# Low parts of twelve input-projection weight tiles by ScalarE and an adding transfer, and eight conv slices a tile

## The chip, the core and the metric

The kernel runs on one core of a Trainium2 chip. The core has a matrix engine (TensorE, PE in the profile), a vector engine (VectorE, DVE), a scalar engine (ScalarE, ACT), a general engine (GpSimd, POOL), and a sync engine (SyncE, SP) that only issues transfers. Each engine works through its own list of instructions in order; semaphores between them say when an operand is ready or a buffer is free. The metric is the device time of one execution in microseconds (us). The kernel before takes 1417.85 us, the median of three runs from 1417.19 to 1418.00.

## The reference

A hybrid decoder layer over 1024 positions of width 1024, all in float32, cut here to the part that matters:

```
proj = rmsnorm(h) @ w_in            # columns: q 512 | k 512 | v 512 | u 1024
a = diff_attention(rope(q), rope(k), v, lam)      # 4 heads, causal, two softmax maps
c = u[:, :512] * sigmoid(u[:, 512:])              # gate
c = causal_dwconv(c, cv_dw_w) + cv_dw_b           # 512 channels, 31 taps
c = silu(layernorm(c))
h = h + concat([a, c]) @ w_out
h = h + cross_attention(...)                      # 4 heads, 256 memory tokens
h = h + conv_ffn(...)                             # gated, width 2816, 3 taps
return rmsnorm(h)
```

## The kernel before

**Products in three matmuls.** Each float32 operand is split into a part `hi`, rounded to the matrix engine's float32r format, and the rest, `lo = x - hi`. A product is `hi*lo + lo*hi + hi*hi`: three matmuls for each 128 x 128 block of weights and 512 columns (`mm3`, lines 198, 199, 200; the second one is the first to read a weight tile's `lo`).

**Input projection.** Sixteen weight tiles of 128 x 1024 (kind `in`, in the order `in_order`: 12, 8, 0, 1, 13, 9, 2, 3, 14, 10, 4, 5, 6, 7, 15, 11) are loaded from HBM by SyncE into `raw` (three buffers). ScalarE copies `raw` to `whi` (line 181), VectorE writes `wlo = raw - whi` (line 182); `whi` and `wlo` have two buffers each, so tile m+1's cast waits until TensorE has read tile m-1 for the last time. Then come four tiles of v (kind `v`), and the sixteen of the memory's keys and values (kind `kv`), which are multiplied beside the attention. Tiles 12 to 15 and 8 to 11 are the two halves of the conv's input; `gate` and `gated` (lines 489 to 499) multiply them, by a sigmoid on ScalarE. `qk_out` (line 504) takes q and k tiles out of PSUM.

**The conv.** `conv31` (line 352) is a generator for one of four channel tiles: some 50 slices, most of them a VectorE multiply-add of 128 x 512 in place (line 371), and at its start, end and middle lines 369 and 377 to 385. The generators, and that of the rotary tables (`rope_tables`, lines 390 to 449), stand in a list `bg`. `run_bg(NBG)` after each weight tile hands out `NBG` slices in turn, at a lowered priority; what is left is handed out before the attention by `run_bg(1000)`.

**Attention.** TensorE's order is fixed by hand in a loop over 32 units (`scores`, `turn`, `weigh`), with the memory's key and value products as filling work (`mem_kv`, line 613). All of `mem_kv` use one PSUM bank, `mb`: unit u+1 waits until unit u has been taken out of it, for the keys by VectorE at line 628. `qk_split` (line 667) splits each head's q and k into `hi` and `lo` (casts on ScalarE at lines 220 and 682, subtractions on VectorE at lines 221 and 683). The first head's split stands ahead of the loop. `maxima` (line 708) and `expo` (line 714) are the softmax.

**What sets the order.** TensorE's instructions keep the order of the code in the stretches under `manual_schedule`. The other engines' lists are put in order when the program is built, from priorities and estimated durations, and are fixed after that; so an edit at one line can shift others on the same engine.

Of the kernel before, what the change touches and what calls it, by code (L numbers as in the profile page):

```python
# [14 lines left out]
ALU = mybir.AluOpType  # L15
# [42 lines left out]
def hybrid_block_kernel(ctx: ExitStack, tc: tile.TileContext, xT, memT, pos, vecs, lams, ropec,  # L58
                        wi, wv, wo, wq, wkv, wc, wu, wd, gfin, outT, outB):
    nc = tc.nc  # L60
# [15 lines left out]
    def nm(s):  # L76
        cnt[0] += 1
        return f"{s}_{cnt[0]}"

    def R():  # L80
        return pt.tile([P, S], F32R, tag="t", name=nm("r"))
# [4 lines left out]
    def T(dt=F32):  # L86
        return pt.tile([P, S], dt, tag="t", name=nm("t"))
# [19 lines left out]
    def f(ap):  # L107
        return ap.bitcast(F32)
# [34 lines left out]
    in_order = [12, 8, 0, 1, 13, 9, 2, 3, 14, 10, 4, 5, 6, 7, 15, 11]  # L143
# [30 lines left out]
    def split_w():  # L174
        kind, m, mode, raw = loaded.pop(0)
        if mode == "rd":
            hi, lo = R(), R()
        else:
            hi = pw[0].tile([P, S], F32R, tag="whi", name=nm("whi"), bufs=2)
            lo = pw[0].tile([P, S], F32R, tag="wlo", name=nm("wlo"), bufs=2)  # L180
        nc.scalar.copy(out=hi, in_=raw)  # L181
        nc.vector.tensor_tensor(out=lo, in0=raw, in1=f(hi), op=ALU.subtract)  # L182
        prepped[(kind, m)] = (hi, lo)

    def need(kind, m, ahead=None):
# [5 lines left out]
    def load_to(i):  # L191
        while wpos[0] <= min(i, wend[0] - 1):
            load_w()
            split_w()
# [65 lines left out]
    for i in range(2):  # L260
        kind, m, src, _ = seq[wpos[0]]
        wpos[0] += 1
        raw = pw[0].tile([P, S], F32, tag="raw", name=nm("raw"), bufs=3)
# [67 lines left out]
    def run_bg(n):  # L331
        with tc.high_priority(offset=-500):
            while n > 0 and bg:
                g = bg.pop(0)
                if next(g, StopIteration) is not StopIteration:
                    bg.append(g)
                    n -= 1
# [117 lines left out]
    def rope(tiles):  # L455

        r = T()
        for h in range(NH):
            nc.scalar.dma_start(out=r[h * 32:(h + 1) * 32, :], in_=tiles[h][48:80, :])
        sw = T()  # L460
        nc.vector.stream_shuffle(out=sw, in_=r, mask=SWAP)
        nc.vector.tensor_tensor(out=r, in0=r, in1=cos_t, op=ALU.mult)
        nc.vector.tensor_tensor(out=sw, in0=sw, in1=sin_t, op=ALU.mult)
        nc.vector.tensor_tensor(out=r, in0=r, in1=sw, op=ALU.add)
        for h in range(NH):
            nc.scalar.dma_start(out=tiles[h][48:80, :], in_=r[h * 32:(h + 1) * 32, :])
# [38 lines left out]
                                           in1=rxb[:, sl], op0=ALU.mult, op1=ALU.mult)  # L505
        qk[m] = t

    NBG = 6

    with tc.manual_schedule(engines={mybir.EngineType.PE}):  # L510
        w, w2 = need("in", 12), need("in", 8, 0)
# [27 lines left out]
    for m in in_order[3:]:  # L539
# [6 lines left out]
        else:  # L546
            qk_out(m, [(slice(0, S), ps)])
            if m % 4 == 3:
                rope(qk[m - 3:m + 1])
        run_bg(NBG)  # L550
    vsb = [T() for _ in range(4)]

    def vproj():
# [3 lines left out]
        for i in range(4):  # L557
# [8 lines left out]
            if i < 3:  # L566
                run_bg(NBG)
        for tb in range(NB):
# [277 lines left out]
    next(prep)  # L846
    run_bg(NBG)

# [139 lines left out]
    for m in range(8):  # L988
# [8 lines left out]
        hi, lo = R(), R()  # L997
# [601 lines left out]
```

## Time and profile before

| | |
|---|---|
| median of three runs | 1417.85 us (1417.19 to 1418.00) |
| the profiled execution | 1418.36 us, of which its span is 1416.6 us |
| TensorE busy | 1378.1 us, 97% of the span |
| VectorE busy | 1066.8 us, 75% |
| ScalarE busy | 578.1 us, 41% |
| GpSimd busy | 211.2 us, 15% |
| mean granted TensorE clock | 0.994 of full speed |

The profile is of one execution. Busy shares are means over the whole span; stages differ much, so the rows further down are cut by stage. `PEclk` is the share of full speed that TensorE was granted in a stretch: 1.00 is 2.4 GHz and 0.50 is 1.2 GHz. In a timeline, the bracket behind a row is the idle time of that engine just before it and what ended that time. Matmuls overlap, so their durations may add up to more than the stretch they lie in. A name such as `cv` or `wlo` stands for all buffers of that name.

### The profile page before, as it was taken

How to read it: one execution, taken by the hardware profiler on the slowest of the kernel's cores; microseconds unless marked ns; L12 is line 12 of the kernel's file. 1: busy time of each engine (PE TensorE's matmuls, PEld its weight loads, DVE VectorE, ACT ScalarE, POOL GpSimd, SP SyncE). 2: the span in 40 equal slices, each digit the busy share in tenths (PEclk: the TensorE clock that was granted, in tenths of full speed). 3: DMA queues.
4: the chain of work that ended last, by engine and by line, in shares of the span. 5: the costliest groups of instructions: out<-in, count | busy, mean ns of one | idle time of the engine just before them, and what ended most of it. 6: DMA issues, size and time to landing. Idle time of an engine off the chain costs nothing.

```text
span 1416.6 us, 17449 instructions
## 1 busy us (share of the span) xinstructions
PE 1378.1 (97%) x6709; PEld 1148.2 (81%) x6709; DVE 1066.8 (75%) x1385; ACT 578.1 (41%) x1023; POOL 211.2 (15%) x169
## 2 busy tenths in 40 slices
PE   8999999898899999999999999999999999999998
PEld 6888887887787888888878787887887877888886
DVE  7799999999955424454688888988888897666636
ACT  6211135688763223343464444444443451221213
POOL 0000000013210000000134333443334400000000
PEclk9999999999999999999999999999999999999999
DMA  6132123432205422202421222222222274313103
GB/s 220 42 98 73 56 90 98 141 118 77 74 31 200 149 90 74 75 31 75 155 80 70 76 80 83 89 75 79 85 75 89 89 299 176 119 61 118 45 1 119
DMA packets 50196, 137.36 MB, mean 97 GB/s; under 512 B 6336, under 2 KB 8640, under 8 KB 50112
## 3 DMA queue, kind: packets, MB, share of 16 engines
q1 hardware_dynamic: 43904, 119.98, 25.2%
q10 hardware_dynamic: 6208, 16.26, 3.6%
q8 instruction: 53, 0.87, 0.2%
q14 instruction: 31, 0.25, 0.1%
HBM read 101.51 MB, written 28.41 MB: 92 GB/s over the span
## 4 chain that ended last, share of the span: by engine, by line
PE 61%; DVE 18%; issue 8%; ACT 7%; POOL 6%; DMA 1%; SPq 0%; POOLq 0%; ACTq 0%; DVEq 0%
PE big L198 16%; PE big L200 16%; PE big L199 16%; POOL t L1171 5%; DVE q L1323 4%; ACT q L1321 3%; PE tb L765 2%; DVE r L221 2%; PE bk L198 1%; DVE wu L221 1%; PE bk L200 1%; PE bk L199 1%; PE mb L198 1%; DVE q L1346 1%; DVE q L1298 1%
## 5 line engine op out<-in xcount | busy, mean ns | idle before, releaser
L199 PE MATMUL big<-r,wlo 128*128 128x512 f32 x624 | 243.7, 390 | 0.6 <-DVE wlo L182 0.6
L200 PE MATMUL big<-r,whi 128*128 128x512 f32 x624 | 243.7, 391 | 0.0
L198 PE MATMUL big<-r,whi 128*128 128x512 f32 x560 | 219.7, 392 | 3.1 <-DVE r L304 2.1
L181 ACT CAST whi<-raw 128x1024 fp32r<-128x1024 f32 x58 | 61.4, 1058 | 204.1 <-PE big L200 171.2
L199 PEld LDWEIGHTS big<-r,wlo 128*128 128x128 f32 x624 | 117.6, 188 | 24.8 <-DVE wlo L182 0.9
L200 PEld LDWEIGHTS big<-r,whi 128*128 128x128 f32 x624 | 117.4, 188 | 24.6
L1431 DVE TENSOR_TENSOR t<-t,big 128x1024 f32<-128x1024 f32 x70 | 85.4, 1220 | 61.9 <-PE big L200 61.8
L1323 DVE SCALAR_TENSOR_TENSOR q<-q,vec,q 128x1023 f32<-128x1023 f32 x88 | 112.6, 1280 | 19.9 <-ACT q L1321 19.8
L198 PEld LDWEIGHTS big<-r,whi 128*128 128x128 f32 x560 | 105.6, 189 | 27.0 <-DVE r L304 3.4
L198 PE MATMUL big<-r,r 128*128 128x512 f32 x312 | 121.8, 391 | 1.8 <-DVE t L1431 1.6
L199 PE MATMUL big<-r,r 128*128 128x512 f32 x312 | 121.5, 389 | 0.0
L200 PE MATMUL big<-r,r 128*128 128x512 f32 x312 | 121.5, 389 | 0.0
L198 PE MATMUL ub<-r,wu 128*128 128x512 f32 x302 | 119.0, 394 | 1.7 <-ACT half L1278 1.7
L199 PE MATMUL ub<-r,wu 128*128 128x512 f32 x302 | 117.6, 389 | 0.0
L200 PE MATMUL ub<-r,wu 128*128 128x512 f32 x302 | 117.6, 389 | 0.0
L1171 POOL TENSOR_TENSOR t<-uraw 128x512 f32<-128x512 f32 x22 | 48.4, 2199 | 389.3 <-DMA uraw<-in_wu_dram 167.1
L198 PE MATMUL ub<-r,t 128*128 128x512 f32 x228 | 90.0, 395 | 4.2 <-ACT half L1278 2.8
L199 PE MATMUL ub<-r,t 128*128 128x512 f32 x228 | 88.8, 390 | 0.0
L200 PE MATMUL ub<-r,t 128*128 128x512 f32 x228 | 88.8, 389 | 0.0
L371 DVE SCALAR_TENSOR_TENSOR cv<-t,vec,cv 128x511 f32<-128x511 f32 (+14 forms) x120 | 84.2, 743 | 0.0
L181 ACT CAST r<-raw 128x1024 fp32r<-128x1024 f32 x22 | 22.9, 1051 | 134.8 <-PE big L198 134.5
L182 DVE TENSOR_TENSOR wlo<-raw,whi 128x1024 fp32r<-128x1024 f32 x58 | 70.9, 1223 | 6.8 <-ACT whi L181 6.6
(340 smaller groups left out, 3047.8 us busy)
## 6 DMA issues: line engine op xcount, KB each, us to landing
uraw<-in_wu_dram SPq DMA_DIRECT2D x88, 256.0 KB, 2.9
z_dr<-q SPq DMA_DIRECT2D x22, 512.0 KB, 2.6
raw<-in_wd_dram SPq DMA_DIRECT2D x22, 512.0 KB, 3.7
t<-z_dr SPq DMA_DIRECT2D x22, 512.0 KB, 4.8
raw<-in_wkv_dram SPq DMA_DIRECT2D x16, 512.0 KB, 3.7
raw<-in_wi_dram SPq DMA_DIRECT2D x14, 512.0 KB, 3.7
t<-h_dr SPq DMA_DIRECT2D x9, 512.0 KB, 10.0
kv_dr<-r SPq DMA_DIRECT2D x8, 512.0 KB, 3.5
```

Of the source, the lines that this page charges most:

```text
L181: nc.scalar.copy(out=hi, in_=raw)
L182: nc.vector.tensor_tensor(out=lo, in0=raw, in1=f(hi), op=ALU.subtract)
L198: nc.tensor.matmul(out, wh, xl, start=start, stop=False, **kw)
L199: nc.tensor.matmul(out, wl, xh, start=False, stop=False, **kw)
L200: nc.tensor.matmul(out, wh, xh, start=False, stop=stop, **kw)
L221: nc.vector.tensor_tensor(out=lo, in0=src, in1=f(hi), op=ALU.subtract)
L371: nc.vector.scalar_tensor_tensor(out=y[:, i:], in0=x[:, :n2 - i], scalar=t, in1=y[:, i:], op0=ALU.mult, op1=ALU.add)
L765: nc.tensor.matmul(av, u["at"][:, bs(j)], vsb[j // 2][:, (j % 2) * HALF + h * P:][:, :P], start=j == 0, stop=j == qb)
L1171: nc.gpsimd.tensor_tensor(out=out, in0=a, in1=b, op=ALU.add)
L1321: nc.scalar.mul(t, u, tp[2])
L1323: nc.vector.scalar_tensor_tensor(out=t[:, d:], in0=u[:, :S - d], scalar=tp[2 - d], in1=t[:, d:], op0=ALU.mult, op1=ALU.add)
L1431: nc.vector.tensor_tensor(out=h2[m], in0=h2[m], in1=ps, op=ALU.add)
```

## The change

For the twelve `in` tiles behind the first four of `in_order`, the subtraction on VectorE goes. ScalarE writes minus `hi` into `wlo` (line 184), and a transfer that GpSimd issues (line 185) adds `raw` to it in place. The first four `in` tiles, and all tiles of other kinds, keep the subtraction. `NBG` goes from 6 to 8.

```diff
@@ -179,7 +179,12 @@
             hi = pw[0].tile([P, S], F32R, tag="whi", name=nm("whi"), bufs=2)
             lo = pw[0].tile([P, S], F32R, tag="wlo", name=nm("wlo"), bufs=2)
         nc.scalar.copy(out=hi, in_=raw)
-        nc.vector.tensor_tensor(out=lo, in0=raw, in1=f(hi), op=ALU.subtract)
+        if kind == "in" and m not in in_order[:4]:
+
+            nc.scalar.mul(lo, f(hi), -1.0)
+            nc.gpsimd.dma_start(out=f(lo), in_=raw, accum_op=ALU.add)
+        else:
+            nc.vector.tensor_tensor(out=lo, in0=raw, in1=f(hi), op=ALU.subtract)
         prepped[(kind, m)] = (hi, lo)
@@ -505,7 +510,7 @@
-    NBG = 6
+    NBG = 8
```

Five lines are added, so what stands at line 220 before is at line 225 after. TensorE's and SyncE's lists hold the same instructions (one weight load of SyncE's moves behind the loads of the rotary tables); GpSimd's gains the twelve transfers in a row, between its two small powers for the statistics (line 231 before). VectorE's and ScalarE's lists change in order too, at two places that matter here.

On VectorE, where the attention begins, the list before has conv slices (`cv_212`, line 371) between the splits of q and k (`r` and `q`, lines 221 and 683), the weights' subtractions (`wlo`) and the copy out of `mem_kv`'s bank (`half`, line 628):

```order
L371 SCALAR_TENSOR_TENSOR cv_212<-t_1269,tsum,cv_212 128x511
L229 TENSOR_SCALAR s_1633<-bk_1624 128x2
L182 TENSOR_TENSOR wlo_1787<-raw_1784,whi_1786 128x1024
L371 SCALAR_TENSOR_TENSOR cv_212<-t_1269,tsum,cv_212 128x510
L221 TENSOR_TENSOR r_1766<-q_445,r_1764 64x1024
L683 TENSOR_TENSOR r_1761<-q_1003,r_1761 64x1024
L371 SCALAR_TENSOR_TENSOR cv_212<-t_1269,tsum,cv_212 128x509
L683 TENSOR_TENSOR r_1762<-q_1003,r_1762 64x1024
L182 TENSOR_TENSOR wlo_1817<-raw_1814,whi_1816 128x1024
L683 TENSOR_TENSOR q_2220<-q_1066,q_2220 64x1024
L371 SCALAR_TENSOR_TENSOR cv_212<-t_1269,tsum,cv_212 128x508
L628 TENSOR_TENSOR half_1781<-mb_1783,rmb 128x512
```

The list after has the conv's last slices there, and then the same work without any:

```order
L376 SCALAR_TENSOR_TENSOR cv_212<-t_1304,tsum,cv_212 128x498
L376 SCALAR_TENSOR_TENSOR cv_212<-t_1304,vec,cv_212 128x497
L226 TENSOR_TENSOR r_1777<-q_445,r_1775 64x1024
L234 TENSOR_SCALAR s_1678<-bk_1669 128x2
L187 TENSOR_TENSOR wlo_1799<-raw_1796,whi_1798 128x1024
L226 TENSOR_TENSOR r_1778<-q_445,r_1776 64x1024
L688 TENSOR_TENSOR r_1773<-q_1025,r_1773 64x1024
L688 TENSOR_TENSOR r_1774<-q_1025,r_1774 64x1024
L187 TENSOR_TENSOR wlo_1829<-raw_1826,whi_1828 128x1024
L688 TENSOR_TENSOR q_2232<-q_1091,q_2232 64x1024
L633 TENSOR_TENSOR half_1793<-mb_1795,rmb 128x512
```

Fifteen slices of the fourth conv tile stand behind the first split of q before, and none after.

On ScalarE, around the fourth of the twelve tiles, the list before has the two sines of the rotary tables (`t_505`, lines 437 and 438) behind that tile's cast (`whi_683`):

```order
L181 CAST whi_614<-raw_612 128x1024
L493 ACTIVATE t_587<-t_587 128x1024
L181 CAST whi_683<-raw_681 128x1024
L437 ACT_TABLE_LOAD
L437 ACTIVATE t_505<-t_505 128x64
L438 ACTIVATE t_505<-t_505 128x64
L459 DMA t_801<-q_445 32x1024
L181 CAST whi_746<-raw_744 128x1024
```

The list after has each tile's cast followed by the multiplication by -1 (`wlo`, line 184), and the second sine stands between the fourth tile's two:

```order
L181 CAST whi_627<-raw_625 128x1024
L184 ACTIVATE wlo_628<-whi_627 128x1024
L498 ACTIVATE t_596<-t_596 128x1024
L442 ACT_TABLE_LOAD
L442 ACTIVATE t_506<-t_506 128x64
L181 CAST whi_692<-raw_690 128x1024
L443 ACTIVATE t_506<-t_506 128x64
L184 ACTIVATE wlo_693<-whi_692 128x1024
L464 DMA t_814<-q_445 32x1024
L181 CAST whi_758<-raw_756 128x1024
```

So `wlo_693` waits for that sine, and the sine for VectorE. On VectorE, in the same place of the program, the list before has what the second sine reads (`t_505`, the second line 433 of the tables) behind the copy-out of the second gate tile (line 498, which waits for TensorE's end of that tile):

```order
L498 TENSOR_TENSOR t_587<-big_618,t_587 128x1024
L371 SCALAR_TENSOR_TENSOR cv_209<-t_440,vec,cv_209 128x497
L182 TENSOR_TENSOR wlo_684<-raw_681,whi_683 128x1024
L431 TENSOR_TENSOR t_505<-t_505 128x64
L439 TENSOR_SCALAR t_505<-t_505 128x64
L369 TENSOR_SCALAR cv_210<-t_587,vec 128x512 x2
L377 TENSOR_TENSOR t_440<-t_440 128x512
L432 TENSOR_SCALAR t_505<-t_505 128x64
L371 SCALAR_TENSOR_TENSOR cv_210<-t_587,vec,cv_210 128x511 x2
L379 SCALAR_TENSOR_TENSOR t_440<-cv_209,vec 128x512
L433 TENSOR_SCALAR t_505<-t_505 128x64
```

The list after has it ahead of that copy-out (now lines 438 and 503):

```order
L376 SCALAR_TENSOR_TENSOR cv_209<-t_440,vec,cv_209 128x497
L436 TENSOR_TENSOR t_506<-t_506 128x64
L444 TENSOR_SCALAR t_506<-t_506 128x64
L382 TENSOR_TENSOR t_440<-t_440 128x512
L437 TENSOR_SCALAR t_506<-t_506 128x64
L384 SCALAR_TENSOR_TENSOR t_440<-cv_209,vec 128x512
L438 TENSOR_SCALAR t_506<-t_506 128x64
L503 TENSOR_TENSOR t_596<-big_632,t_596 128x1024
```

So the second sine no longer stands behind TensorE's end of that tile.

## Rows read from the trace of the kernel before

**Rows 1.** The page, part 1: the span; each engine's busy time, share, instructions.

```profile
span 1416.6 us, 17449 instructions
PE 1378.1 (97%) x6709; PEld 1148.2 (81%) x6709; DVE 1066.8 (75%) x1385; ACT 578.1 (41%) x1023; POOL 211.2 (15%) x169
```

**Rows 2.** Windows: us, busy PE, PEld, DVE, ACT, POOL (instructions), PEclk, DMA share, GB/s.

```profile
60.00:187.00 127.00, 127.00 (x562) 105.17 (x561) 122.95 (x185) 24.36 (x30) 0.00 (x0) 1.00 0.29 80
...
231.00:259.00 28.00, 22.20 (x153) 20.93 (x152) 27.28 (x37) 16.90 (x24) 2.28 (x1) 0.88 0.50 148
259.00:311.00 52.00, 50.54 (x402) 47.06 (x401) 47.75 (x83) 40.01 (x102) 5.52 (x12) 1.00 0.45 138
311.00:400.00 89.00, 78.63 (x594) 70.28 (x594) 81.08 (x165) 73.44 (x204) 22.57 (x43) 0.98 0.24 70
```

**Rows 3.** Timeline of TensorE: start, duration, instruction; idle before and its end.

```profile
243.69 0.37 PE L198 MATMUL mb<-r,whi 128*128 128x256 f32 x1 [3.48 <-DVE half L628]
...
255.13 0.55 PE L198 MATMUL mb<-r,whi 128*128 128x256 f32 x1 [2.32 <-DVE s L734]
...
266.65 0.39 PE L198 MATMUL mb<-r,whi 128*128 128x256 f32 x1 [0.67 <-DVE half L628]
...
327.77 0.66 PE L822 MATMUL tb<-ident,half 128*128 128x128 f32 x4 [1.56 <-ACT junk L770]
```

**Rows 4.** Groups by shape, VectorE, 48 to 173 us: count, busy us, mean ns.

```profile
L182 DVE TENSOR_TENSOR wlo<-raw,whi 128x1024 fp32r<-128x1024 f32 x12 | 14.7, 1222 | 0.0
```

**Rows 5.** Timeline of VectorE from 231 to 269 us, five of its rows.

```profile
231.38 1.22 DVE L221 TENSOR_TENSOR r<-q,r 64x1024 fp32r<-64x1024 f32 x1 [1.76 <-ACT r L220]
232.52 0.74 DVE L371 SCALAR_TENSOR_TENSOR cv<-t,tsum,cv 128x511 f32<-128x511 f32 x1
...
242.86 0.69 DVE L628 TENSOR_TENSOR half<-mb,rmb 128x512 f32<-128x512 f32 x1
...
254.30 0.69 DVE L628 TENSOR_TENSOR half<-mb,rmb 128x512 f32<-128x512 f32 x1
...
268.36 0.73 DVE L371 SCALAR_TENSOR_TENSOR cv<-t,vec,cv 128x497 f32<-128x497 f32 x1
```

**Rows 6.** Timeline of ScalarE: casts, a sine, and the casts of the first splits.

```profile
85.63 0.26 ACT L438 ACTIVATE t<-t 128x64 f32<-128x64 f32 x1 [4.19 <-DVE t L433]
...
89.70 1.06 ACT L181 CAST whi<-raw 128x1024 fp32r<-128x1024 f32 x1 [3.82 <-PE big L200]
...
100.58 1.05 ACT L181 CAST whi<-raw 128x1024 fp32r<-128x1024 f32 x1 [9.82 <-PE big L200]
...
233.97 2.13 ACT L682 CAST r<-q 64x1024 fp32r<-64x1024 f32 x2
```

**Rows 7.** Groups on ScalarE, 48 to 173 us: the sigmoid's mean ns, 128 x 1024.

```profile
L493 ACT ACTIVATE t<-t 128x1024 f32<-128x1024 f32 x2 | 2.1, 1065 | 1.1 <-DVE t L491 1.1
```

**Rows 8.** Transfers: tensors, queue, count, KB each, median us from issue to landing.

```profile
raw<-in_wi_dram SPq DMA_DIRECT2D x14, 512.0 KB, 3.7
...
t<-h_dr SPq DMA_DIRECT2D x9, 512.0 KB, 10.0
...
r<-r SPq DMA_DIRECT2D x14, 256.0 KB, 3.0
```

**Rows 9.** Windows, as rows 2: one behind each of two waits.

```profile
245.00:247.00 2.00, 2.00 (x12) 2.00 (x11) 1.97 (x2) 0.92 (x2) 0.00 (x0) 0.50 0.14 27
...
327.00:331.00 4.00, 3.15 (x22) 2.66 (x23) 3.30 (x10) 4.00 (x14) 2.24 (x4) 1.00 0.04 10
```

**Rows 10.** TensorE's waits, 311 to 400 us: total us, times, longest us.

```profile
PE tb L822 <- ACT t L753: 2.8, 1, 2.8
...
PE tb L752 <- DVE t L738: 1.4, 1, 1.4
...
PE tb L822 <- DVE r L224: 1.2, 1, 1.2
```

**Rows 11.** VectorE's waits, 60 to 231 us: total us, times, longest us.

```profile
DVE q L504 <- PE big L200: 3.1, 4, 1.2
```

## The prediction

> **What bounds the kernel now.** I read the page first: TensorE is busy 97% of a span of 1416.6 us [rows 1], so a change to another engine can win only where TensorE waits or is slowed, and lose only where it makes TensorE wait. The profiled execution took 1418.36 us, 1.8 more than its span and 0.5 more than the median of the runs, 1417.85. Then I read the windows by stage [rows 2]. In the input projection, where all twelve edited tiles lie, TensorE is busy 127.00 of 127 us at a granted clock of 1.00, and VectorE 122.95. Nothing can be won there: VectorE is full, but TensorE does not wait for it. The next window, 231 to 259 us, is where the attention begins. There TensorE is busy 22.20 of 28 us and its clock is 0.88, while VectorE is busy 27.28. From 259 to 311 us TensorE loses 1.5 us, from 311 to 400 us 10.4 us.
>
> The timeline of TensorE shows what the 5.8 us are [rows 3]: two waits, 3.48 us up to 243.69 and 2.32 us up to 255.13, both before the first matmul of a memory unit into the bank `mb`. The first ends with line 628, the copy-out of that bank on VectorE. The second is put down to an instruction at 254.90 that starts as line 628 ends (254.30 + 0.69 = 254.99) [rows 5], so it is the same wait. VectorE reaches line 628 late, since its list between 231.38 and 268.36 us holds fifteen slices of the conv, of which the first and the last are shown [rows 5]. After a wait the clock falls: 0.50 from 245 to 247 us [rows 9]. In the whole window it is 0.88, which costs 28 x 0.12 = 3.4 us [rows 2]. Shorter waits did not do that: after the 1.56 us up to 327.77 the clock is 1.00 [rows 3, 9].
>
> **What the change removes.** Twelve subtractions of 1.22 us, 14.7 us of VectorE's time [rows 4]. None of it lies on the path where it is taken out. What counts is what fills the room: the conv's slices. Fifteen slices at some 0.7 us from start to start are about 10.5 us, less than the 14.7, so there is room for all of them ahead of the attention; in the new order none stands behind the first split of q. NBG = 8 is only how they are let forward; I cost it at nothing by itself.
>
> **What that is worth at 231 to 259 us.** From the split at 231.38 to line 628 at 242.86 VectorE's list holds four slices, 2.9 us from start to start. I take 2.6, since the instructions left still read casts that end up to 236.1 on ScalarE (233.97 + 2.13) [rows 6]. So the first wait shrinks from 3.48 to 0.9 us. Before the second line 628 stand more slices than that wait is long; it can shrink to what the copy-out alone costs, 0.67 us, as up to 266.65 [rows 3]. I take 0.9, a gain of 1.4. Both waits are then shorter than 1.56 us, so the clock should stay up. I take 3.0 of the 3.4 us, as some of the slow stretch lies in the waits themselves. Sum: 2.6 + 1.4 + 3.0 = 7.0 us.
>
> After 259 us I count nothing: the waits there mostly end with ScalarE or GpSimd, the longest of 2.8 us with ScalarE [rows 10], no slice stands in them after 268.36, and they move forward as a whole. Bounds: 2.6 us if only the first wait shrinks and the clock falls as before; 9.5 us if the two waits that end with VectorE, 1.2 and 1.4 us [rows 10], go as well (7.0 + 2.5).
>
> **What the change adds, and its cover.** Twelve multiplications on ScalarE, priced by an activation of the same shape at 1.06 us [rows 7], 12.8 us; ScalarE is busy 24.36 of 127 us there [rows 2], so they are hidden unless they are in the chain of a tile. They are: cast, multiplication, transfer, and then TensorE's second matmul of the tile. The chain starts when TensorE releases a buffer (the cast at 89.70) and must end one tile later (100.58) [rows 6]. The tile is 10.9 us, less two instructions of 1.06 us and 0.2 us for handovers; the transfer may take **8.5 us**.
>
> No row shows an adding transfer or one that GpSimd issues, so its duration D is bounded. Below: 3.7 us, a load of the same 512 KB; a copy inside SBUF of half the bytes takes 3.0 [rows 8]. Above: 10.0 us, the slowest row of 512 KB [rows 8]. It reads two operands where a copy reads one, so I take twice the load, 7.4 us: 1.1 us of cover left, cost 0. Beyond 8.5 a tile waits D - 8.5, and only every second tile does, since the next tile's chain started a tile earlier than its turn: six waits. At 10.0 us that is 6 x 1.5 = 9 us. GpSimd's list is empty there, so nothing queues behind the twelve; the third `raw` buffer is held some 7 us longer of the 33 that three tiles take, so loads aren't late.
>
> The Trainium skill has a price too: "DMA: Bandwidth & Descriptors", section "Anatomy of one DMA", gives about 2.0 us plus bytes by 436 GB/s, which would be an estimated 3.2 us here, and "Collectives: The Full Stack", section "The bandwidth ceiling", says that an added transfer is slow by its two source reads, not by the adding. By both D would be about 4.4 us and the cost 0 as well; no run here shows it.
>
> One tile more: the fourth tile's multiplication now stands behind the second sine of the rotary tables. Before, that sine ran at 85.63 after waiting 4.2 us for VectorE [rows 6]. At that time the tile would be ready at 85.63 + 0.26 + 1.06 + 7.4 = 94.4, where TensorE wants it at about 89.9: 4.5 us, once. In the new order VectorE does the sine's operand ahead of the copy-out, not behind, so I take 0 of 0 to 4.5.
>
> **The sum.** 1418.4 - 7.0 = 1411.4, half a microsecond less on the scale of the runs: **1411 us**. A difference under 0.2%, 2.8 us, I call none, since a measurement of this kernel can tell little less.
>
> **Rivals.** *Late transfers (slower).* The place is the twelve tiles, the price 6 x (D - 8.5) us. From D = 9.7 it eats the 7 us, from 10.2 the kernel is measurably slower. At 12 us it is 21 - 7 = 14: 1432 us. For it: 10.0 us occurs for 512 KB, and issue by GpSimd is unpriced. Against: the median loads of this size are at 3.7, and the DMA share in the stage is only 0.29 [rows 2].
>
> *Starved descriptors (slower still).* VectorE is 97% busy in the stage, and waits for TensorE seldom (3.1 us in four waits at line 504) [rows 11, 2]. If GpSimd can't prepare a transfer while VectorE works, each is put off to VectorE's next pause, about half a tile: 5.4 + 7.4 = 12.8 us, 6 x 4.3 = 26 us, about 1437. The Trainium skill ("SBUF — State Buffer", section "SBUF: two separate sides") says that VectorE's instructions that take both port pairs keep GpSimd from writing descriptors; by its list only single-input kinds do, few here, so it speaks for little. The rows show neither.
>
> *The gain is given back.* From 311 to 400 us TensorE waits 10.4 us, most of it for ScalarE [rows 2, 10]. If ScalarE, not TensorE, paces this stretch, an earlier start is waited off and the time stays at 1415 to 1420, say 1417. Against: ScalarE is busy 73 of 89 us, and its work hangs on TensorE's.
>
> *More.* All of VectorE's 10.5 us reach TensorE, with the clock's 3: some 1406.
>
> **Chances.** Forecast 0.60 (1408.5 to 1415), given back 0.13, late 0.17, starved 0.05, more 0.05. Faster by over 0.2%: 0.60 + 0.05 = 0.65. Within: 0.13 + 0.02 of the late case with D of 9.3 to 10.2 = 0.15. Slower: 0.15 + 0.05 = 0.20. The range is 1406 to 1424: it takes in the forecast, given back, most of more, and late up to D = 10.6 (6 x 2.1 - 7 = +5.6); some 0.16 stay out above.
>
> **What would show it.** Right: no conv slice after about 232 us, TensorE without a wait in the projection, the two waits near 0.9 us each, the clock at 1.00 from 239 to 259 us, and later waits as before. Wrong: TensorE's line for the second matmul of a tile waiting for a transfer in the projection, about every second tile; a transfer of more than 8.5 us from issue to landing; a slice left behind 232 us; or a saving at 259 us that is gone at 400 us.

## The result, and the profile after

The changed kernel takes 1410.05 us (median of four runs, 1409.63 to 1412.24) where the kernel before takes 1417.86 beside it. The ratio is 0.9949, with a 95% interval from 0.9932 to 0.9966: 7.2 us less, from 4.8 to 9.6. Its profiled execution took 1410.40 us with a span of 1408.6, 8.0 less than before. In the page, TensorE's busy time falls by 2.6 us (it counts matmuls that run at the lower clock) and its idle time by 5.4. One later execution, of the kernel notr, took 2306.42 us at a granted clock of 0.556 and is left out of the numbers below.

The span and each engine's busy time, from the page of the changed kernel:

```profile
span 1408.6 us, 17491 instructions
PE 1375.5 (98%) x6709; PEld 1146.8 (81%) x6709; DVE 1058.6 (75%) x1373; ACT 590.2 (42%) x1035; POOL 220.5 (16%) x181
```

Its windows by stage (us, busy PE, PEld, DVE, ACT, POOL, then PEclk, DMA share, GB/s), which answer to [rows 2]:

```profile
60.00:187.00 127.00, 127.00 (x562) 105.15 (x561) 117.86 (x179) 32.23 (x35) 8.62 (x10) 1.00 0.52 124
187.00:231.00 44.00, 44.00 (x204) 36.74 (x203) 42.53 (x60) 15.82 (x23) 0.00 (x0) 1.00 0.21 63
231.00:259.00 28.00, 25.34 (x186) 23.65 (x186) 25.59 (x32) 19.07 (x30) 1.64 (x1) 0.94 0.61 181
259.00:311.00 52.00, 49.38 (x394) 45.95 (x392) 45.97 (x86) 42.12 (x111) 6.15 (x13) 1.00 0.39 120
311.00:400.00 89.00, 79.83 (x592) 71.16 (x592) 78.62 (x161) 73.11 (x202) 23.44 (x43) 0.98 0.23 69
```

TensorE still doesn't wait in the projection. From 231 to 259 us it is busy 25.34 us instead of 22.20, at a clock of 0.94 instead of 0.88. Its timeline there, which answers to [rows 3]:

```profile
240.04 0.38 PE L203 MATMUL mb<-r,whi 128*128 128x256 f32 x1 [1.79 <-DVE half L633]
250.06 0.36 PE L203 MATMUL mb<-r,whi 128*128 128x256 f32 x1 [0.88 <-DVE s L739]
260.21 0.38 PE L203 MATMUL mb<-r,whi 128*128 128x256 f32 x1 [0.67 <-DVE half L633]
...
321.33 0.66 PE L827 MATMUL tb<-ident,half 128*128 128x128 f32 x4 [1.55 <-ACT junk L775]
```

These four rows and those of [rows 3] cut the 8.0 us into pieces. Before, TensorE first stops for `mb` at 243.69 - 3.48 = 240.21 us, after at 240.04 - 1.79 = 238.25: 1.96 us were won earlier. From that stop to the matmul that ends the third wait it is 26.44 us before (to 266.65) and 21.96 after: 4.48 us, the piece that the prediction is about. From there to the wait of 1.56 (1.55) us it is 61.12 us in both. The last 1.56 us come behind that point: 1088.83 us to the end of the span before, 1087.27 after.

VectorE at the same place, which answers to [rows 5]:

```profile
229.94 0.73 DVE L376 SCALAR_TENSOR_TENSOR cv<-t,vec,cv 128x497 f32<-128x497 f32 x1
230.59 1.21 DVE L226 TENSOR_TENSOR r<-q,r 64x1024 fp32r<-64x1024 f32 x1
...
238.05 1.22 DVE L688 TENSOR_TENSOR q<-q,q 64x1024 fp32r<-64x1024 f32 x1
239.30 0.69 DVE L633 TENSOR_TENSOR half<-mb,rmb 128x512 f32<-128x512 f32 x1
```

The last conv slice now stands ahead of the first split, as the order said. But the split has no idle time ahead of it, where it had 1.76 us before [rows 5]: VectorE comes to it straight from the slices. ScalarE's timeline says how late; its first two rows are the chain of one of the twelve tiles (the cast, then the multiplication):

```profile
87.87 1.05 ACT L181 CAST whi<-raw 128x1024 fp32r<-128x1024 f32 x1 [8.72 <-PE big L205]
88.95 1.06 ACT L184 ACTIVATE wlo<-whi 128x1024 fp32r<-128x1024 f32 x1
...
228.54 1.03 ACT L225 CAST r<-q 64x1024 fp32r<-64x1024 f32 x1
```

The split's cast is done at 229.57, the split starts at 230.59, 1.02 us late. The transfer of the same tile on GpSimd, and then the group of all twelve from the list of transfers (count, KB each, median us from issue to landing):

```profile
90.31 0.86 POOL L185 DMA_DIRECT2D wlo<-raw  x1 [10.00 <-ACT wlo L184]
```

```profile
wlo<-raw POOLq DMA_DIRECT2D x12, 512.0 KB, 4.6
```

The 4.6 us are a median; this one transfer, in the view of `wlo` from 90 to 91.2 us, takes longer:

```profile
DMA to landing us min/median/max: 6.1/6.1/6.1
```

It lands at about 90.31 + 6.1 = 96.4 us. ScalarE's next cast, which waits for TensorE's end of the tile between, is at 98.75: over 2 us of cover are left. The slowest of the twelve takes 7.1 us, which is still less than the 8.5 of the prediction.

### The profile page after: what moved, and what is told of

Read it like the earlier page. It is cut to its first block, busy times and chain, and to the rows that moved or that the text cites. A ratio compares the mean times of both kernels' runs of the same rounds, so it can differ in the third digit from the quotient of the medians.

```text
span 1408.6 us, 17491 instructions
## 1 busy us (share of the span) xinstructions
PE 1375.5 (98%) x6709; PEld 1146.8 (81%) x6709; DVE 1058.6 (75%) x1373; ACT 590.2 (42%) x1035; POOL 220.5 (16%) x181
## 4 chain that ended last, share of the span: by engine, by line
PE 58%; DVE 21%; issue 8%; ACT 7%; POOL 4%; DMA 2%; SPq 0%; ACTq 0%; POOLq 0%; DVEq 0%
PE big L203 14%; PE big L205 14%; PE big L204 14%; DVE q L1328 4%; POOL t L1176 4%; ACT q L1326 3%; DVE cv L376 2%; PE tb L770 2%; DVE r L226 2%; DVE t L226 1%; DVE q L1351 1%; DVE wu L226 1%; PE bk L203 1%; PE ub L203 1%; PE bk L205 1%
## 5 line engine op out<-in xcount | busy, mean ns | idle before, releaser
L181 ACT CAST r<-raw 128x1024 fp32r<-128x1024 f32 x22 | 22.9, 1052 | 134.8 <-PE big L203 134.5
L1176 POOL TENSOR_TENSOR t<-t,uraw 128x512 f32<-128x512 f32 x44 | 72.3, 1643 | 3.4
```

The costliest lines, as they stand in the source:

```text
L1176: nc.gpsimd.tensor_tensor(out=out, in0=a, in1=b, op=ALU.add)
```

## The experiments

All were timed in five rounds against the kernel before, in three batches, in which that took 1416.73, 1415.18 and 1416.48 us. "The stretch" is the time from TensorE's first stop before `mb` to the matmul that ends its third wait there, 26.44 us before and 21.96 after. Single runs of one kernel differ by up to 6 us (the kernel before: 1413.76 to 1419.62), so the stretch tells more than the medians.

**ctl: the kernel before, moved by five lines.**

```diff
+(five blank lines behind line 182)
```

> The kernel before with five blank lines, nothing else. Theory A (the 7.8 us of the change are some 4.5 us at the attention's start, 231 to 259 us, and the rest is chance: 2.0 us at the first loads, where the clock was 0.97 before and 1.00 after over 0 to 60 us, and 1.3 us in the FFN's small waits, 4.5 us in 15 before and 2.6 us in 9 after): time as before, 1417 to 1418.5, but the profile differs from that of before at these two places by 1 to 2 us either way. Theory B (the change made these two gains as well): the profile shows both places as before, 0.97 and some 4.5 us.

1417.49 us, ratio 1.0003 [0.9994, 1.0013]. The stretch is 26.20 us, the waits 3.48 and 2.35. The clock over the first loads is 0.93 again, and the FFN's small waits for line 1278 (1283 here) are 4.0 us in 13. By itself that spoke for theory B; the next two told otherwise for the start.

**nbg8: before with NBG = 8.**

```diff
-    NBG = 6
+    NBG = 8
```

> Before with NBG = 8 and no transfer. Theory A (VectorE's time is what was short, and the number only lets slices forward): no room is made, ten slices still stand behind the first split of q, the two waits before mb stay near 3.5 and 2.3 us, 1417 to 1418.5. Rival (handing slices out earlier is the gain): the slices are gone from there and the time is 1411 to 1414.

1416.72 us, ratio 1.0000 [0.9991, 1.0008]. The stretch is again 26.20 us, and fifteen slices, not ten, stand behind the first split of q. TensorE's waits in it:

```profile
241.86 0.55 PE L198 MATMUL mb<-r,whi 128*128 128x256 f32 x1 [3.48 <-DVE half L628]
253.29 0.36 PE L198 MATMUL mb<-r,whi 128*128 128x256 f32 x1 [2.38 <-DVE s L734]
258.05 0.66 PE L752 MATMUL tb<-ident,t 128*128 128x128 f32 x4 [0.72 <-DVE t L738]
264.58 0.39 PE L198 MATMUL mb<-r,whi 128*128 128x256 f32 x1 [0.88 <-DVE half L628]
```

The number does nothing by itself. This kernel has no transfer, and yet it comes to its first stop as early as the changed one, at 238.38. The windows from 0 to 24 us of before, of nbg8, of the changed kernel and of aft (the changed kernel again, below):

```profile
0.00:24.00 24.00, 20.42 (x73) 14.27 (x74) 17.06 (x30) 18.77 (x27) 1.09 (x8) 0.93 0.86 297
```

```profile
0.00:24.00 24.00, 21.37 (x83) 15.28 (x84) 17.11 (x30) 18.85 (x27) 1.08 (x8) 1.00 0.87 297
```

```profile
0.00:24.00 24.00, 21.22 (x83) 15.12 (x84) 17.06 (x30) 18.70 (x27) 1.08 (x8) 1.00 0.87 295
```

```profile
0.00:24.00 24.00, 20.18 (x73) 14.28 (x74) 16.55 (x30) 18.21 (x26) 1.07 (x8) 0.93 0.86 294
```

The clock column is 0.93 or 1.00 without the transfers and 1.00 or 0.93 with them, the last two in one and the same kernel. So the 1.96 us ahead of the first stop are not the change's; they go with the first loads and the clock there, which differ from one execution to the next. Over the eleven profiles in which no transfer is waited for, the first stop is at 239.32 to 240.21 us where the clock is 0.93, and at 238.25 to 238.82 where it is 1.00, except in six (240.84), which stays unexplained.

**nbg6: the transfers alone.**

```diff
-    NBG = 8
+    NBG = 6
```

> After with NBG = 6 again: the transfers alone. Theory A: no slice behind the first split of q, and the time of after, 1409.5 to 1411. Rival (the larger number is needed): slices return behind the split and 2 to 5 us of the gain go, 1412 to 1415.

1410.85 us, ratio 0.9960 [0.9945, 0.9974]. The stretch is 20.84 us, shorter than in the changed kernel:

```profile
241.12 0.39 PE L203 MATMUL mb<-r,whi 128*128 128x256 f32 x1 [1.80 <-DVE half L633]
250.02 0.36 PE L203 MATMUL mb<-r,whi 128*128 128x256 f32 x1 [1.28 <-ACT whi L181]
260.16 0.38 PE L203 MATMUL mb<-r,whi 128*128 128x256 f32 x1 [0.67 <-DVE half L633]
```

The first wait is the same as in the changed kernel, 1.80 against 1.79 us, but the clock stayed at 1.00 behind it. Without its waits the stretch is 20.84 - 3.75 = 17.09 us here, 21.96 - 3.34 = 18.62 in the changed kernel's profile and 26.44 - 6.47 = 19.97 before. The changed kernel's profile thus lost 1.5 us to the clock, before 2.9. In ctl and nbg8, where the clock fell behind the first wait only, there are four waits, as in the rows of nbg8, and it is 26.20 - 7.43 = 18.77 and 26.20 - 7.46 = 18.74: 1.7 us lost, but 1 us more of waits than in before.

**notr: no transfer.**

```diff
-            nc.gpsimd.dma_start(out=f(lo), in_=raw, accum_op=ALU.add)
```

> After with the twelve adding transfers left out, so wlo holds minus hi there and the output isn't the reference's. Theory A (each transfer, 4.6 us to landing, is hidden behind 10.9 us of a tile, and disturbs nothing): within 1 us of after, 1409 to 1411. Rival (the transfers slow loads, VectorE or the first matmuls): 1405 to 1408.

1410.37 us, ratio 0.9954 [0.9938, 0.9970]; the stretch is 20.58 us. The time lies among those of the kernels that have the transfers, so they cost nothing that the times can tell. The stretch is no clean measure of them, since VectorE's list is not the same: the last slice stands behind the first split here (at 231.31 us, the split at 230.17). That the transfers are hidden is told by the changed kernel itself, in which TensorE is busy 127.00 of 127 us.

**aft: the changed kernel again.** No edit.

> The changed kernel itself again, as the measure for the other three. Theory A (its own gain is made at the attention's start alone, 4.5 to 5.9 us from the first wait before mb to 328 us, and what goes beyond is chance of the first loads and the FFN): 1409.5 to 1411.5 and 5 to 7 us below before in this batch. Theory B (7.8 us are its own): 7.5 to 8.2 us below before again.

1411.18 us, ratio 0.9964 [0.9951, 0.9976]: 5.1 us less by the ratio, 4.0 by the medians. The stretch is 20.95 us, with waits of 1.89, 1.27 and 0.68 and a clock of 1.00. The 8.0 us of the first pair of profiles were not all its own.

**kv: the memory's tiles too.**

```diff
-        if kind == "in" and m not in in_order[:4]:
+        if (kind == "in" and m not in in_order[:4]) or kind == "kv":
```

> After, with the sixteen kv tiles made by ScalarE and the transfer too. Theory A (what TensorE still waits for at the attention's start is VectorE's list ahead of the copy-out of mb, in which two subtractions of 1.22 us stand): the first wait goes from 1.8 to 0.7 to 0.9 us, the second to 0.7 to 1.0, the time is 1 to 3 us below the changed kernel. Rival (from 311 to 400 us ScalarE sets the pace, 73 of 89 us, and sixteen times 1.06 us more on it comes out at the end): waits for ScalarE there grow from 7 to 10 us or more, the time is 2 to 6 us above the changed kernel.

1436.31 us, ratio 1.0137 [1.0118, 1.0157]: 25 us above the changed kernel. Neither theory had it. TensorE's longest group of waits, and its windows from 231 us:

```profile
PE mb L204 <- DMA wlo<-raw: 18.8, 7, 4.7
```

```profile
231.00:259.00 28.00, 19.22 (x120) 17.90 (x120) 15.08 (x21) 18.43 (x25) 4.19 (x5) 0.85 0.77 175
259.00:311.00 52.00, 39.66 (x260) 36.26 (x259) 22.57 (x39) 31.89 (x64) 5.94 (x7) 0.86 0.74 181
```

It is the prediction's rival of the late transfers, in a place where it holds. In the changed kernel two kv tiles pass in 260.21 - 250.06 = 10.15 us, 5.1 a tile; less 2.3 for the cast, the multiplication and the handovers, a transfer may take 2.8 us, and it takes 4.9 (median of 28). VectorE is busy only 22.57 of 52 us here, and that helps nothing.

**vkv: the v tiles as well.**

```diff
+        if (kind == "in" and m not in in_order[:4]) or kind in ("v", "kv"):
```

> As kv, and the four v tiles too, which takes 4.9 us more from VectorE's list ahead of the first split of q. Theory A (the conv slices reach VectorE's first split about 1 us late in the changed kernel, since the room made was just short): the split no longer starts late, the waits before mb are at 0.7 us, 0 to 1 us below kv. Rival (the room sufficed; the list order alone sets the first wait): as kv.

1440.37 us, ratio 1.0171 [1.0156, 1.0185]. The waits at the kv tiles cover the question that it was made for. It adds one wait of 4.31 us at the first v tiles, for a transfer that takes 7.1 us and starts late, since its cast (at 180.97 us) and its multiplication (182.87) stand behind other work of ScalarE. The other three v tiles show no wait.

**dbl: two transfers in a row.**

```diff
-            nc.scalar.mul(lo, f(hi), -1.0)
+            nc.scalar.mul(lo, f(hi), -2.0)
+            nc.gpsimd.dma_start(out=f(lo), in_=f(hi), accum_op=ALU.add)
             nc.gpsimd.dma_start(out=f(lo), in_=raw, accum_op=ALU.add)
```

> After with minus twice hi from ScalarE and two transfers in a row, the first adding hi, the second raw: the same lo, one transfer later. Theory A (a transfer may take 8.5 us; one takes about 4.6 to 5.5 us from issue to landing, so two take 9.2 to 11 and every second tile waits 0.7 to 2.5 us): six waits for wlo in the projection, 4 to 15 us above the changed kernel, 1414 to 1425. Rival (the cover is longer than worked out, or the two overlap): no wait, the time of the changed kernel.

1433.48 us, ratio 1.0114 [1.0096, 1.0133]: 22 us above the changed kernel, past the upper end of theory A. TensorE's waits in the projection, its window, and GpSimd's two groups (count, busy us and mean ns, idle before):

```profile
PE big L205 <- DMA wlo<-raw: 16.5, 9, 6.5
```

```profile
60.00:187.00 127.00, 114.86 (x480) 92.02 (x478) 101.11 (x161) 24.52 (x25) 16.34 (x19) 0.95 0.68 145
```

```profile
L185 POOL DMA_DIRECT2D wlo<-whi x12 | 10.7, 891 | 65.6 <-ACT wlo L184 65.6
L186 POOL DMA_DIRECT2D wlo<-raw x12 | 10.3, 860 | 70.9 <-DMA wlo<-whi 70.9
```

From one issue to the next it is (70.9 + 10.7) / 12 = 6.8 us, and the second lands 4.5 us later: 11.3 in all. The prediction's price gives 6 x (11.3 - 8.5) = 16.8 us, and the waits are 16.5. That the two agree is partly chance: the waits come in nine pieces, not six, and one of them is 6.5 us (before 101.27 us), behind two transfers that took 7.7 and 8.2 us. That there are waits at 11.3 us and none at 4.6 to 7.1 fits a cover of 8.5, but does not measure it. The clock of 0.95 over 127 us adds 6.4, which the price left out: 22.9, and TensorE's first stop before `mb` comes 263.47 - 239.95 = 23.5 us later than in aft. So a late transfer can be paid twice, in waiting and in clock, though not always: the clock is 0.84 to 0.93 from 60 to 126 us, behind waits of 2.46 and 6.46, and 1.00 from 126 to 214, where the waits are at most 1.88 us.

**six: the last six tiles only.**

```diff
-        if kind == "in" and m not in in_order[:4]:
+        if kind == "in" and m in in_order[10:]:
```

> After, but the transfer makes only the last six of the in tiles; the other ten keep the subtraction, which leaves 7.3 of the 14.7 us of VectorE's time. In its order six slices stand behind the first split of q, three of them ahead of the first copy-out of mb, where before has fifteen and four and after none. Theory A (what counts is how many slices stand among the splits): first wait near 2.8 us, second near 1.5 to 2, some 23 to 24.5 us from TensorE's first stop before mb to the third matmul unit there (26.2 to 26.4 before, 20.6 to 22.0 with the twelve), so 2 to 4 us below before. Rival (the late tiles' room is what serves the fourth conv tile, the early ones' is lost): the waits and time of after.

1413.15 us, ratio 0.9982 [0.9973, 0.9991]: 2.6 us below before by the ratio, as theory A had it. The stretch is 25.26 us, above the 23 to 24.5 expected:

```profile
243.62 0.35 PE L203 MATMUL mb<-r,whi 128*128 128x256 f32 x1 [2.78 <-DVE half L633]
254.43 0.36 PE L203 MATMUL mb<-r,whi 128*128 128x256 f32 x1 [3.22 <-DVE half L633]
266.10 0.38 PE L203 MATMUL mb<-r,whi 128*128 128x256 f32 x1 [0.67 <-DVE half L633]
```

The first wait is the 2.8 us expected. The second is 3.22 and not 1.5 to 2. The window between the two shows the reason:

```profile
244.00:255.00 11.00, 7.78 (x63) 7.25 (x63) 10.88 (x16) 6.78 (x13) 0.00 (x0) 1.00 0.34 119
```

The clock stayed at 1.00 behind the first wait. So TensorE came to its second stop 251.21 - 243.62 = 7.59 us after the first wait's end, where it took 252.81 - 243.69 = 9.12 before, and VectorE still had slices there. A gain of clock ahead of a wait is in part waited off.

**v23: two v tiles more.**

```diff
+        if (kind == "in" and m not in in_order[:4]) or (kind == "v" and m >= 2):
```

> After, with the third and fourth v tile made by the transfer too: 2.4 us less on VectorE between 187 and 231 us. Theory A (VectorE reaches the first split 1.1 us after its cast is done, because the slices just don't fit): the split starts on time; since one more subtraction of a q split (1.22 us) now stands ahead of the copy-out of mb, the first wait stays at 1.7 to 2.0 us, the second becomes shorter, and the stretch up to the third unit is 0 to 1 us shorter; time 0 to 1 us below the changed kernel, no wait for a transfer at the v tiles (10.9 us each). Rival (v's lo is read by the first matmul of a tile, so the cover is shorter): waits for wlo of 1 to 4 us as at the first v tile of vkv, 1 to 8 us above.

1409.59 us, ratio 0.9951 [0.9939, 0.9964]; no wait for a transfer. The stretch is 20.06 us. VectorE at the first split, and TensorE's waits:

```profile
228.15 0.74 DVE L376 SCALAR_TENSOR_TENSOR cv<-t,vec,cv 128x497 f32<-128x497 f32 x1
229.89 1.22 DVE L226 TENSOR_TENSOR r<-q,r 64x1024 fp32r<-64x1024 f32 x1 [1.01 <-ACT r L225]
```

```profile
239.55 0.38 PE L203 MATMUL mb<-r,whi 128*128 128x256 f32 x1 [1.01 <-DVE half L633]
248.46 0.36 PE L203 MATMUL mb<-r,whi 128*128 128x256 f32 x1 [1.27 <-ACT whi L181]
258.60 0.38 PE L203 MATMUL mb<-r,whi 128*128 128x256 f32 x1 [0.67 <-DVE half L633]
```

Now VectorE waits for its cast, and the first wait is 1.01 us, near the 0.9 of the prediction. My expectation named 1.7 to 2.0, since I took one more q split to stand ahead of line 633. It had only changed places with a weight tile's subtraction (line 187).

**ord and cut2: the same room by other means.**

```diff
-    in_order = [12, 8, 0, 1, 13, 9, 2, 3, 14, 10, 4, 5, 6, 7, 15, 11]
+    in_order = [12, 8, 0, 1, 13, 9, 2, 3, 14, 10, 4, 5, 15, 11, 6, 7]
```

```diff
-        yield from chain(yo, xe, [tap_sum(i) for i in range(1, 16)], 1)
+        yield from chain(yo, xe, [tap_sum(i) for i in range(1, 14 if ct == 3 else 16)], 1)
```

> After, with tiles 15 and 11 (the fourth conv tile's) ahead of 6 and 7 in in_order, so that its slices may begin 22 us earlier. Theory A: as v23, the first split starts on time and 0 to 1 us is won at the attention's start, not more, as what is left there are VectorE's splits themselves. Rival (k's last tiles come too late for the rotation and the second head's split): new waits behind 231 us, 1 to 5 us above the changed kernel.

> After, with the last two slices of the fourth conv tile left out (1.5 us of VectorE's work right ahead of the first split; the conv's result isn't the reference's). Theory A (VectorE is 1.1 us late there): the first split starts where its cast ends; since the order again puts one more q split ahead of the copy-out, the first wait is 1.7 to 2.0 us and the stretch to the third unit is 0 to 1 us shorter. Rival (lateness of VectorE is all of the 1.8 us over the copy-out's own 0.7): the first wait falls to 0.7 to 0.9 us and the stretch by 1 us or more.

ord 1410.62 us, ratio 0.9957 [0.9943, 0.9971]; cut2 1410.99, ratio 0.9960 [0.9947, 0.9972]. Both have a stretch of 20.06 us and a first wait of 1.01 us, as v23. Three different ways to bring VectorE to the split in time give the same stretch to a hundredth, 0.8 to 0.9 us less than nbg6 and aft. In cut2 the rival was nearer with its 0.7 to 0.9 us for the wait. In the medians 0.8 us is too little to see: v23 has the lowest one, but its interval overlaps both of the changed kernel's (0.9932 to 0.9966, 0.9951 to 0.9976), so it can't be called faster.

## Why the prediction was right

- **The mechanism was the right one.** The slices that stood among the splits of q and k went ahead of them into the room of the twelve subtractions. With six tiles part of the stretch was won, with NBG alone nothing, with the transfers alone all of it.
- **First wait: 2.6 us taken, 1.7 measured** (3.48 to 1.79). The step that failed is "there is room for all of them ahead of the attention". It set 10.5 us of slices against 14.7 us removed. But the fourth conv tile's slices can only start when its gate is done, at about 190 us, and from 187 to 231 VectorE is busy 42.53 of 44 us. Much of the room lay earlier, where VectorE now waits (117.86 busy of 127, before 122.95). The last slice ends some 1 us late, and v23, ord and cut2 take just that away.
- **Second wait: 1.4 us taken, 1.4 in the profile (2.32 to 0.88), 1.0 to 1.1 in nbg6 and aft**, where TensorE comes sooner because of the clock.
- **Clock: 3.0 us taken of 3.4; 1.4 in the changed kernel's profile (2.9 lost before, 1.5 after).** In nbg6 and aft nothing is lost, which is 2.9 us against the profile of before, but 1.7 against ctl and nbg8. So the term hangs on which executions are compared, and it doesn't simply add to the waits: nbg6 lost 1.5 us less than the changed kernel's first profile, and its stretch is 1.1 shorter, since its second wait is longer. The waits were held to be shorter than one of 1.56 us that left the clock alone [rows 3, 9]; the first was 1.79, and then the clock falls in one execution and not in two others.
- **Sum for the attention's start: 7.0 us taken.** The stretch is 26.2 to 26.4 us in before, ctl and nbg8, and 20.8 to 22.0 in the changed kernel and nbg6: 4.2 to 5.6. The mechanism held, with a size some fifth to two fifths smaller than taken.
- **Gain given back: no.** The 61.1 us behind the stretch are the same in all of them.
- **Transfers: 7.4 us taken between 3.7 and 10.0, 4.6 measured (4.5 to 7.1), cost 0 as forecast.** The estimate of 4.4 us from the Trainium skill ("Collectives: The Full Stack", section "The bandwidth ceiling", with the fit of "DMA: Bandwidth & Descriptors", section "Anatomy of one DMA") was nearer than my doubling of a load. It doubles the bytes and not the fixed part; whether that is the reason, transfers of a single size can't show. Nor were descriptors starved, which the Trainium skill ("SBUF — State Buffer", section "SBUF: two separate sides") lays to VectorE instructions that take both port pairs: with VectorE busy 117.86 of 127 us eleven of GpSimd's twelve rows are at 0.85 to 0.87 us, the first at 1.23. The second sine's one-off cost was 0, as taken: TensorE doesn't wait there.
- **The total is nearer than its parts, and that is luck.** Of the first pair's 8.0 us, 4.5 are the piece forecast at 7.0; 2.0 are the chance of the first loads (nbg8 and aft), and 1.6 come from behind the stretch, where nothing was forecast. The second measurement, aft, gives 5.1 us less by the ratio.
- **Left open:** behind the wait at 321 to 328 us, the three kernels without the change take 1088.8 to 1090.0 us to their end and the eight with it, or with part of it, 1086.6 to 1088.1. That is 1 to 2 us in the FFN's small waits and in the clock from 311 to 400 us (0.96 to 1.00), though the lists of VectorE, ScalarE and GpSimd are the same there in all but notr and six. Each part alone overlaps between the two groups. Theory A called this chance; the profiles don't settle it.

## What to carry to other kernels

Room on an engine counts only in the stretch in which the work that is to fill it may start: set freed time against moved time between the moment the moved work is ready and the moment it is due, not over the whole stage. A transfer that replaces an instruction was free here where its whole chain, cast, multiplication and transfer, was shorter than one tile of the engine that reads it: 10.9 us a tile hid it, 5.1 us did not. And when single executions differ by as much as the effect, compare the stretch between two landmarks in the traces; at equal clock it repeated here to 0.1 us (20.84 and 20.95 us in nbg6 and aft, 26.20 in ctl and nbg8).

## What the hardware showed that I had not expected

The clock behind a wait is not a function of the wait alone: behind 1.79 us it fell (0.94 over 231 to 259 us), behind 1.80 and 1.89 us it stayed at 1.00, in one and the same place of the program. In six it stayed at 1.00 even behind 2.78 us (244 to 255 us). Behind the second wait of the kernels without the change it fell to 0.50 after 2.32 us (before, 256 to 258 us) and stayed at 1.00 after 2.35 (ctl, 255 to 259 us). What decides it, the traces don't show. And two adding transfers in a row on the same tile are not twice one: the first took 6.2 us from issue to landing (median of 12, up to 13.0), where single ones take 4.6. The traces don't show why; in both kernels the slowest ones are issued between 79 and 97 us (7.1 and 13.0).
